# Two-layer hybrid encoder, 1 core: meta queries of mixer D stacked into fewer products, mixer A's sums of squares moved behind the next transpositions, rotation read from SBUF, last columns stored in two pieces

## Chip, cores and metric

The kernel runs on one core of a Trainium2 chip. The metric is the device time of the program in microseconds (us), the median of several executions. TensorE is called PE here, VectorE DVE, ScalarE ACT, GpSimd POOL, SyncE SP.

## What is computed

A trunk of two layers over 272 tokens (16 meta tokens ahead of 256 inputs, whose rows alone are put out) with a width of 1024, all in float32. Cut to what the change touches:

```python
u = rms_norm(h, g_pre)                       # per layer
(a_q, a_k, a_v, b_..., c_..., d_q, d_k, d_v, gate_logits) = split(u @ w_in)
# A: differential attention, 4 heads of 2 x 64, values of 128
#    p = softmax(q k' / 8 + bias), one map per m
#    o = (p[0] - lam * p[1]) @ v ; o = rms_norm(o, subln) * (1 - lam_init)   per head
# B: gated linear attention, in chunks
# C: latent attention, 4 heads of 128 + 64; the 64 are rotated:
#    rope(x) = [x1 * cos - x2 * sin, x1 * sin + x2 * cos]
# D: 8 query heads of 64 on 2 key heads, band of +-128, 16 meta tokens seen by all and seeing all,
#    one sink logit per head
merged = sum_i (branch_i @ w_branch_i) * sigmoid(gate_i)
h = h + rms_norm(merged @ w_out, g_post)
h = h + rms_norm(conv_ffn(rms_norm(h)), g_ffn_post)      # returned: h[:, 16:]
```

## The kernel before, in words

**Products.** Activations lie transposed, 128 features on the partitions and the 272 tokens along the free axis. Every product is made three times on split operands (`mm3`, L305): high times high, high times low, low times high, each part rounded to fp32r. Weights come by DMA on SP's queue as tiles `raw` of 128x1024 (three buffers); ACT rounds each to `wh` and DVE subtracts to get `wl` (both L221), two tiles ahead of their use (five buffers). A projection is a run of 24 matmuls `pj` per 128 output rows, into one of three PSUM banks ("mm").

**Order of work.** Per layer the mixers A, B, C, D follow one another. While one mixer's steps are computed, projections of the next mixer, gates and branch products (`br`) are put between its steps as filling, so many per step by a table. Attention heads are staggered: scores of head h (first half of the queries), transpositions for head h-1, scores of head h (second half), products with the values for head h-1. A Tile scheduler then fixes an order for each engine; each engine works its list in that order, so that a waiting instruction holds all behind it. The other PSUM banks are two for scores ("sc") and three for the rest ("ax": transpositions `tpv`, `tpp`, `tpr`, `tpm`, sums `ps_A`, outputs `poA`). In layer 1 the last layer's unneeded meta rows are left out, so 258 columns instead of 272 stand in many of its instructions.

**Meta queries.** The 16 meta tokens' queries of all heads go through one score tile `scm` (128 rows = heads x 16). For that, `fill_qm` (L584) copies the queries into a zeroed tile, `QM`, high part in `Ah` and low part in `Al` (ACT copy and DVE subtraction, L311 and L312). In D (`comp_d`, L1151) four such blocks are multiplied by `mm3` each: 12 matmuls (L1160 to L1162). The softmaxed rows `pm` are then transposed by `m_transposed` (L645) into `tpm`: three matmuls in float32 against the identity for C and D, where a float32 matmul appears as two records in the trace. All other transpositions (`PE.transpose`, L186) have one record.

**A.** `values(h)` (L947) begins with `head_sums(h-1)`: two matmuls `ps_A` with a matrix of ones that sum the squares of head h-1's outputs, and ACT's copy of them to `aq` (L945). Then come `tpv` (values), `tpp` and `tpr` (maps), ACT's and DVE's splitting of those to `pth`, `ptl`, `ptr`, `vh`, `vl`, `vrA`, and, after filling, the products `poA`. ACT copies `poA` to `av` (L960), squares and rounds it (L520, L521), DVE makes the low part. `scores(h)` (L924) begins with `q_split` of its queries.

**C's rotation.** `rope` (L977) is called for a PSUM bank `qu`: ACT scales the bank to `cq` (L1042), copies four groups of 32 partitions from the bank, swapped and scaled, to `sw` (L983; one buffer), DVE multiplies `sw` by the sines (L984) and `cq` by the cosines (L985), and adds (L986).

**End.** The last down-projection accumulates in four banks `dt`. For the last 128 rows, per half of 512 columns: ACT squares and sums (L1337), DVE multiplies by the gain to `yt` (L1338). Then DVE adds the two sums (L1339), ACT takes Ln and Exp (L1340, L1341, shown as L163), DVE scales and adds the residual per half (L1344), and each half is stored, one from SP's queue, one from ACT's (L1345).

Of the kernel before, what the change touches and what calls it, by code (L numbers as in the profile page):

```python
# [13 lines left out]
F32 = mybir.dt.float32  # L14
F32R = mybir.dt.float32r
AF = mybir.ActivationFunctionType
# [4 lines left out]
P = 128  # L21
# [96 lines left out]
def hybrid_kernel(ctx: ExitStack, tc: tile.TileContext, hT0, w, pc_in, p2_in, cc_in, oh_in, tab_in, gl_in, out):  # L118
# [142 lines left out]
    for nm, wd in (("Ah", 640), ("Al", 640), ("R", P)):  # L261
        QM[nm] = const.tile([P, wd], F32R, name=f"qm{nm}")
        G.memset(QM[nm].bitcast(F32), 0.0)
    keep_warm(N_WARM0)
    PTR = []
    VR = {}
    for i in range(2):
# [205 lines left out]
    for l in range(DEPTH):  # L473
# [9 lines left out]
        with ExitStack() as scope:  # L483
# [161 lines left out]
            def m_transposed(pm, rhs, ncols, name):  # L645
                tm = tmp.tile([P, 3, P], F32, name=name, tag="tm", bufs=1)
                tp = axb("tpm")
                for kc, (k0, n) in enumerate(KC):
                    PE.matmul(tp[:n, kc * ncols:(kc + 1) * ncols], lhsT=pm[:, k0:k0 + n], rhs=rhs, start=True,
                              stop=True)  # L650
                V.tensor_copy(tm[:, 0:2, :ncols], tp[:, :2 * ncols].rearrange("p (a b) -> p a b", a=2))
                V.tensor_copy(tm[:16, 2, :ncols], tp[:16, 2 * ncols:3 * ncols])
                return tm
# [242 lines left out]
            def comp_a(d):  # L896
# [21 lines left out]
                pm, st = softmax_rows(psm, biasMA, -NEG)  # L918
                V.tensor_mul(st[:, 1:2], st[:, 1:2], lamM)
                V.tensor_scalar(pm, pm, st[:, 1:2], None, ALU.mult)  # L920
                yield
                tm, sqs = [], []

                def scores(h, pair):  # L924
                    bias = tmp.tile([P, 2, 400], F32, name="bA", tag="bias")
                    toep(bias, 2 * h, -RMAX, P, 400, [[ROW, 2]])
                    qh, ql = q_split(d["q"][h])
                    for qt in range(2):
                        pp = []
                        for m in range(2):  # L930
                            r = slice(64 * m, 64 * m + 64)
                            qr = slice(128 - 128 * qt, 256 - 128 * qt)
                            ps = scb("sc")
                            mm3(ps[:, :T], qh[r, qr], ql[r, qr], ak[0][h][r, :], ak[1][h][r, :], True, True)
                            off = 128 * (1 - qt)
                            pp.append(softmax_rows(ps, bias[:, m, off:off + T], -NEG))
                        (p0, s0), (p1, s1) = pp
                        V.tensor_mul(s1[:, 1:2], s1[:, 1:2], neglam)
                        V.tensor_scalar(p0, p0, s0[:, 1:2], None, ALU.mult)
                        V.scalar_tensor_tensor(p0, p1, s1[:, 1:2], p0, ALU.mult, ALU.add)  # L940
                        pair.append(p0)
                        yield

                def head_sums(h):
                    S.copy(d["q"][h][:, cs], sum_heads(sqs[h], "A")[:, cs])  # L945

                def values(h, pair):  # L947
                    if h:
                        head_sums(h - 1)
                    else:  # L950
                        tm.append(m_transposed(pm, C("comb"), 64, "tmA"))
                    e = slice(h * P, (h + 1) * P)
                    vh, vl = v_transposed(d["v"][h], VR["A"][:, e])
                    pts = pt_tiles()
                    transpose_p(pts, pair)
                    put_m(pts, tm[0], 16 * h)
                    yield
                    po = axb("poA")
                    pv(po, lambda kc: vh[:, kc, :], lambda kc: vl[:, kc, :], VR["A"][:, e], pts, True, True)
                    S.copy(d["v"][h][:, cs], po[:, cs])  # L960
                    sqs.append(square_hl(d["v"][h]))
# [12 lines left out]
                    yield  # L974


            def rope(dst, src, rows, c0=0, scale=1.0):  # L977

                sw = tmp.tile([P, T], F32, name="sw", tag="sw", bufs=1)
                c = slice(c0, T)  # L980
                for b_ in range(0, rows, 32):
                    o = b_ ^ 32
                    S.activation(sw[b_:b_ + 32, c], src[o:o + 32, c], AF.Copy, scale=scale)  # L983
                V.tensor_mul(sw[:rows, c], sw[:rows, c], C("sin", 0, rows)[:, c])  # L984
                V.tensor_mul(dst[:, c], dst[:, c], C("cos", 0, rows)[:, c])  # L985
                V.tensor_add(dst[:, c], dst[:, c], sw[:rows, c])  # L986

            def proj_c(d, kper):
                lf, sqs = [], []
                for n in (1, 2):  # L990
                    yield from proj_f(n, "cl", lf, None, ct * (n - 1))
                    sqs += [square(f, f"sqc{n}", ct * (n - 1)) for f in lf[n - 1:]]
                rope(kper, kper, 64)
                kp = u("kph", F32R), u("kpl", F32R)
                split(kp[0][0:64, :], kp[1][0:64, :], kper)
                S.copy(kp[0][64:128, :], kper)
                V.tensor_sub(kp[1][64:128, :], kper, kp[0][0:64, :].bitcast(F32))
                d["kp"], d["lat"] = kp, (lf, sqs)
                yield
# [19 lines left out]
            def proj_c_up(d):  # L1019
# [16 lines left out]
                for i in (4, 5, 0, 1, 2, 3):  # L1036
                    ps = mmb("qu")
                    for k in range(2):
                        mm3(ps[:, cs], wq[k][0][:, i * P:(i + 1) * P], wq[k][1][:, i * P:(i + 1) * P], lh[1 + k][:, cs],
                            ll[1 + k][:, cs], k == 0, k == 1)  # L1040
                    qf.append(u(f"cq{i}"))
                    S.activation(qf[-1][:, cs], ps[:, cs], AF.Copy, scale=C_SCALE)  # L1042
                    if i >= 4:
                        rope(qf[-1], ps, P, ct, C_SCALE)
                    if i % 2:
                        yield
                qf[:] = qf[2:] + qf[:2]

            def comp_c(d):
# [43 lines left out]

                def values(h, pair):
                    if not h:
                        tm.append(m_transposed(pm, ident, P, "tmC"))
                    e = slice(h * P, (h + 1) * P)
                    vh, vl = v_transposed(vf[h], VR["A"][:, e])
                    pts = pt_tiles()
# [8 lines left out]
                pairs = [[] for _ in range(4)]  # L1108
                yield from staggered([(scores(h, pairs[h]), values(h, pairs[h])) for h in range(4)])


            def proj_d(d):
                kh, kl = u4("dkh", F32R, 2), u4("dkl", F32R, 2)
# [31 lines left out]
                turn()  # L1145
                d["k"], d["v"], d["q"] = (kh, kl), vp, [u("dq0")]
                evac(dq0, d["q"][0], RS, 0.125, ct)
                yield
                yield from proj_f(3, "dq", d["q"], 0.125, ct)

            def comp_d(d):  # L1151
                dq, (kh, kl), vp = d["q"], d["k"], d["v"]
                clear_qm(0)
                fill_qm("A", dq, 160, 2)
                d["br"] = br = branch_tiles("brD")
                vr = VR["D"].rearrange("p (a b) -> p a b", a=2)
                nsink = sm.tile([P, 9], F32, name="nsink", tag="nsink", bufs=1)
                V.tensor_scalar(nsink, PCc("sink", 0, 9), -1.0, None, ALU.mult)
                psm = scb("scm")
                for j in range(4):  # L1160
                    mm3(psm[:, :T], QM["Ah"][:, j * P:(j + 1) * P], QM["Al"][:, j * P:(j + 1) * P], kh[j // 2],
                        kl[j // 2], j == 0, j == 3)  # L1162
                pm, st = softmax_rows(psm, biasMD, nsink[:, 8:9], sink=PCc("sinkM"))
                V.tensor_scalar(pm, pm, st[:, 1:2], None, ALU.mult)
                yield
                tm, qs, pos = [], [], []

                def scores(hd, pair):
                    j, par = divmod(hd, 2)
                    if not par:  # L1170
                        qs[:] = q_stack(dq[j])
                    kv = hd // 4
                    bias = tmp.tile([P, 2, 400], F32, name="bD", tag="bias")
                    toep(bias[:, :, 0:16], 16 + hd, -271, P, 16, [[128, 2]])
# [1 line left out]
                    for qt in range(2):  # L1176
                        qr = slice(128 - 128 * qt, 256 - 128 * qt)
                        ps = scb("sc")
                        stacked(ps[:, :T], qs[par][:, qr], kh[kv], kl[kv], True, True)
                        p, st = softmax_rows(ps, bias[:, 1 - qt, :T], nsink[:, hd:hd + 1], sink=PCc("sink", hd))  # L1180
                        V.tensor_scalar(p, p, st[:, 1:2], None, ALU.mult)
                        pair.append(p)
                        yield

                def values(hd, pair):
                    j, par = divmod(hd, 2)
                    kv = hd // 4
                    if not hd:
                        tm.append(m_transposed(pm, ident, P, "tmD"))
                    pts = pt_tiles()  # L1190
                    transpose_p(pts, pair)
                    put_m(pts, tm[0], 16 * hd)
# [79 lines left out]
        with tc.tile_pool(name=f"ffn{l}", bufs=1, reuse_waits="tile") as ffn:  # L1272
# [34 lines left out]
            def down_rows():  # L1307
# [17 lines left out]
                for t in range(2):  # L1325
# [3 lines left out]
                    for n in range(2):  # L1329
# [5 lines left out]
                            PE.matmul(ps, lhsT=ah[:, kk, c], rhs=ws[1][:, e], start=False, stop=kk == NF - 1)  # L1335
                        sq = ffn.tile([P, 512], F32, name="sqt", tag="sqt", bufs=2)
                        S.activation(sq, ps, AF.Square, accum_out=st[:, n:n + 1])  # L1337
                        V.tensor_mul(y[:, e], ps, gl[:, e])  # L1338
                    V.tensor_add(st[:, 2:3], st[:, 0:1], st[:, 1:2])  # L1339
                    act(LN_EXP_SET, st[:, 3:4], st[:, 2:3], AF.Ln, scale=1.0 / DM, bias=epst)  # L1340
                    act(LN_EXP_SET, st[:, 3:4], st[:, 3:4], AF.Exp, scale=-0.5)  # L1341
                    for n in range(2):
                        e = slice(512 * n, 512 * n + 512)
                        V.scalar_tensor_tensor(y[:, e], y[:, e], st[:, 3:4], ht[:, t, e], ALU.mult, ALU.add)  # L1344
                        (nc.sync, S)[n].dma_start(out[P * t:P * t + P, e], y[:, e])  # L1345

            ah = ffn.tile([P, NF, T], F32R, name="ah")
            al = ffn.tile([P, NF, T], F32R, name="al")
# [209 lines left out]
```

## Time and profile before

| what | value |
| --- | --- |
| times of three runs | 1138.22, 1136.12, 1136.78 us; median 1136.78 |
| the profiled execution | 1137.86 us, of which the span from first to last instruction is 1136.1 |
| granted clock of TensorE, mean | 0.999 |
| busy in the span | PE 98%, DVE 81%, ACT 67%, POOL 1% |
| weights and other data moved | 183.73 MB, mean 162 GB/s |

The profiled execution took 1.8 us more than its span, and 1.1 us more than the median of the three runs. "Busy" of PE counts overlapping matmuls: while PE runs without a gap, a matmul of 272 columns has a duration of 0.29 us in the trace, but the next one starts 0.125 us later. So the worth of a matmul is read from starts, not from durations.

### The profile page before, as it was taken

The numbers are of one execution on the slowest core, as the hardware profiler recorded it, in microseconds if no ns is written. First come the engines' busy times: TensorE is split into PE (matmuls) and PEld (weight loads), VectorE is DVE, ScalarE is ACT, GpSimd is POOL, SyncE is SP. The second block draws the span as 40 slices with busy tenths as digits, with TensorE's granted clock in tenths as the row PEclk, the third lists the DMA queues.
The fourth block names the chain that finished last, engine by engine and source line by source line (L and its number), as shares of the span: only waits on it lengthen the run. The fifth ranks groups of instructions, "written<-read, shape, count | busy, mean of one in ns | idle before, by whom it ended". The sixth has DMA issues, their size and how long they took to land.

```text
span 1136.1 us, 22808 instructions
## 1 busy us (share of the span) xinstructions
PE 1113.3 (98%) x8678; PEld 1077.5 (95%) x8678; DVE 918.8 (81%) x2001; ACT 760.9 (67%) x1623; POOL 12.8 (1%) x57
## 2 busy tenths in 40 slices
PE   9999999999999999999999999999999999999997
PEld 8999899999999999999999998999999999999986
DVE  6977986898976899995479868868989759999843
ACT  7756787777755767664457557867777657766632
POOL 1000000000000000000000000000000000000000
PEclk9999999999999999999999999999999999999999
DMA  7643444445656356655546434644466472655551
GB/s 266 217 149 117 132 149 149 131 130 135 168 149 214 105 173 202 183 165 175 181 143 214 149 114 126 159 154 136 139 146 173 150 244 93 208 201 186 186 188 71
DMA packets 60914, 183.73 MB, mean 162 GB/s; under 512 B 10443, under 2 KB 17739, under 8 KB 60420
## 3 DMA queue, kind: packets, MB, share of 16 engines
q1 hardware_dynamic: 60148, 181.36, 51.8%
q8 instruction: 68, 1.11, 0.4%
q10 hardware_dynamic: 656, 0.91, 0.2%
q14 instruction: 42, 0.34, 0.1%
HBM read 180.03 MB, written 2.21 MB: 160 GB/s over the span
## 4 chain that ended last, share of the span: by engine, by line
PE 77%; DVE 9%; ACT 8%; DMA 3%; issue 2%; DVEq 0%; SPq 0%; ACTq 0%
PE pj L183 49%; PE br L183 7%; PE dn L183 6%; PE dt L183 5%; DMA raw<-wst 3%; DVE wl L221 2%; ACT wh L221 2%; PE poD L183 1%; PE sc L183 1%; PE poB L183 1%; PE at L183 1%; PE tpp L186 1%; ACT p L607 1%; ACT sw L983 1%; PE kvu L183 1%
## 5 line engine op out<-in xcount | busy, mean ns | idle before, releaser
L183 PE MATMUL pj<-xh,wh 128*128 128x272 f32 (+1 forms) x1888 | 547.2, 292 | 6.4 <-ACT xh L350 3.1
L183 PE MATMUL pj<-xl,wh 128*128 128x272 f32 (+1 forms) x1888 | 540.6, 287 | 0.0
L183 PE MATMUL pj<-xh,wl 128*128 128x272 f32 (+1 forms) x1888 | 540.3, 287 | 0.0
L221 DVE TENSOR_TENSOR wl<-raw,wh 128x1024 fp32r<-128x1024 f32 (+2 forms) x322 | 387.1, 1205 | 111.4 <-ACT wh L221 108.5
L221 ACT CAST wh<-raw 128x1024 fp32r<-128x1024 f32 (+2 forms) x322 | 332.7, 1035 | 198.5 <-PE pj L183 90.8
L183 PEld LDWEIGHTS pj<-xh,wh 128*128 128x128 f32 x1888 | 354.7, 189 | 12.1 <-ACT xh L350 3.7
L183 PEld LDWEIGHTS pj<-xl,wh 128*128 128x128 f32 x1888 | 356.6, 189 | 1.8 <-issue 0.4
L183 PEld LDWEIGHTS pj<-xh,wl 128*128 128x128 f32 x1888 | 355.9, 189 | 0.2
L1365 ACT ACTIVATE cv<-u,pc 128x272 f32<-128x272 f32 (+1 forms) x88 | 52.9, 606 | 15.2 <-DVE u L1363 15.0
L183 PE MATMUL dn<-ah,wh 128*128 128x272 f32 x176 | 51.0, 290 | 0.0
L183 PE MATMUL dn<-al,wh 128*128 128x272 f32 x176 | 50.7, 288 | 0.0
L183 PE MATMUL dn<-ah,wl 128*128 128x272 f32 x176 | 50.5, 287 | 0.0
L607 ACT ACTIVATE p<-p,st 128x272 f32<-128x272 f32 x68 | 35.1, 516 | 14.6 <-DVE st L605 14.5
L1369 DVE SCALAR_TENSOR_TENSOR cv<-u,pc,cv 128x271 f32<-128x271 f32 (+1 forms) x88 | 43.0, 490 | 1.8
L1367 DVE SCALAR_TENSOR_TENSOR cv<-u,pc,cv 128x271 f32<-128x271 f32 (+1 forms) x88 | 42.9, 488 | 1.0 <-ACT cv L1365 0.6
L1210 DVE TENSOR_TENSOR gt<-pj,rs_x 128x272 f32<-128x272 f32 (+1 forms) x64 | 27.6, 431 | 15.2 <-PE pj L183 14.3
L1363 DVE TENSOR_TENSOR u<-pj,rs_x 128x272 f32<-128x272 f32 (+1 forms) x88 | 36.9, 426 | 0.0
L183 PE MATMUL dt<-wh,al 128*128 128x512 f32 x88 | 34.8, 395 | 0.0
L183 PE MATMUL dt<-wh,ah 128*128 128x512 f32 x88 | 34.7, 395 | 0.0
L183 PE MATMUL dt<-wl,ah 128*128 128x512 f32 x88 | 34.5, 392 | 0.0
L183 PEld LDWEIGHTS dn<-ah,wh 128*128 128x128 f32 x176 | 33.1, 188 | 0.0
L183 PEld LDWEIGHTS dn<-al,wh 128*128 128x128 f32 x176 | 33.1, 188 | 0.0
(390 smaller groups left out, 1894.1 us busy)
## 6 DMA issues: line engine op xcount, KB each, us to landing
raw<-wst SPq DMA_DIRECT2D x306, 512.0 KB, 3.7
raw<-wst SPq DMA_DIRECT2D x12, 384.0 KB, 3.2
bD<-bvec SPq DMA_DIRECT2D x16, 256.0 KB, 5.1
bA<-bvec SPq DMA_DIRECT2D x8, 400.0 KB, 5.7
hT<-hT SPq DMA_DIRECT2D x1, 1088.0 KB, 6.3
h_dram<-hT SPq DMA_DIRECT2D x1, 1088.0 KB
hT<-h_dram SPq DMA_DIRECT2D x1, 1088.0 KB, 6.1
raw<-wst SPq DMA_DIRECT2D x4, 256.0 KB, 4.6
```

The source lines that it names most:

```text
L183: self.note(nc.tensor.matmul(*args, **kw))
L186: self.note(nc.tensor.transpose(*args, **kw))
L221: pair = S.copy(wh[:, c], raw[:, c]), V.tensor_sub(wl[:, c], raw[:, c], wh[:, c].bitcast(F32))
L607: S.activation(p, p, AF.Exp, scale=-1.0, bias=st[:, 0:1], accum_out=st[:, 1:2])
L983: S.activation(sw[b_:b_ + 32, c], src[o:o + 32, c], AF.Copy, scale=scale)
L1210: V.tensor_mul(f[:, ct:T], (yield from pj(ct))[:, ct:T], RS[:, ct:T])
L1363: V.tensor_mul(u_[:, ct:T], ps[:, ct:T], RS[:, ct:T])
L1365: S.activation(t[:, cd:T], u_[:, cd:T], AF.Identity, scale=PCc("cw1", c), bias=PCc("cb", c))
L1367: V.scalar_tensor_tensor(t[:, lo:T], u_[:, lo - 1:T - 1], PCc("cw0", c), t[:, lo:T], ALU.mult, ALU.add)
L1369: V.scalar_tensor_tensor(t[:, cd:T - 1], u_[:, cd + 1:T], PCc("cw2", c), t[:, cd:T - 1], ALU.mult, ALU.add)
```

## The change

It has five parts.

1. D's meta queries are stacked: the high and the low part of a query lie above each other in one 128-row block (`QS`, 128 columns of the tile `QM` that were not used), one block for each key head. `meta_q` fills it after each of the four query projections, in place of `fill_qm` at the start of `comp_d`; `stacked` multiplies a block with the high and with the low keys: 4 matmuls instead of 12 per layer.
2. `m_transposed` uses `PE.transpose` for C and D.
3. A's `head_sums(h-1)` goes from the start of `values(h)` to just ahead of `poA`; `q_split` in A and `q_stack` in D are issued a step earlier.
4. `rope` reads `cq`, which lies in SBUF, instead of the PSUM bank.
5. In the end part, the sums are added ahead of the second multiplication by the gain, which is issued after Ln and Exp; the last 512 columns of the last rows are stored as two pieces of 256.

```diff
+    QS = [QM[nm][:, 512:640] for nm in ("Ah", "Al")]
...
                 for kc, (k0, n) in enumerate(KC):
-                    PE.matmul(tp[:n, kc * ncols:(kc + 1) * ncols], lhsT=pm[:, k0:k0 + n], rhs=rhs, start=True,
-                              stop=True)
+                    o = tp[:n, kc * ncols:(kc + 1) * ncols]
+                    if rhs is None:
+                        PE.transpose(o, pm[:, k0:k0 + n], ident)
+                    else:
+                        PE.matmul(o, lhsT=pm[:, k0:k0 + n], rhs=rhs, start=True, stop=True)
...
+                qs = [q_split(d["q"][0])]
                 yield
...
-                    qh, ql = q_split(d["q"][h])
+                    qh, ql = qs.pop()
...
                         pair.append(p0)
+                        if qt and h < 3:
+                            qs.append(q_split(d["q"][h + 1]))
                         yield
...
                 def values(h, pair):
-                    if h:
-                        head_sums(h - 1)
-                    else:
+                    if not h:
                         tm.append(m_transposed(pm, C("comb"), 64, "tmA"))
...
                     put_m(pts, tm[0], 16 * h)
                     yield
+                    if h:
+                        head_sums(h - 1)
                     po = axb("poA")
...
-                    S.activation(sw[b_:b_ + 32, c], src[o:o + 32, c], AF.Copy, scale=scale)
+                    S.copy(sw[b_:b_ + 32, c], dst[o:o + 32, c])
...
+            def meta_q(dq, j):
+
+                for m in range(2):
+                    o = 16 * (2 * (j % 2) + m) + 64 * (j // 2)
+                    oc, t = slice(o, o + 16 - ct), QS[j // 2]
+                    r, r2 = slice(64 * m, 64 * m + 64), slice(64 - 64 * m, 128 - 64 * m)
+                    src = dq[j][r, 15:ct - 1 if ct else None:-1]
+                    S.copy(t[r, oc], src)
+                    V.tensor_sub(t[r2, oc], src, t[r, oc].bitcast(F32))
...
-                yield from proj_f(3, "dq", d["q"], 0.125, ct)
+                for j in range(1, 4):
+                    yield from proj_f(1, f"dq{j}_", d["q"], 0.125, ct)
+                    meta_q(d["q"], j)
...
-                for j in range(4):
-                    mm3(psm[:, :T], QM["Ah"][:, j * P:(j + 1) * P], QM["Al"][:, j * P:(j + 1) * P], kh[j // 2],
-                        kl[j // 2], j == 0, j == 3)
+                for kv in range(2):
+                    stacked(psm[:, :T], QS[kv], kh[kv], kl[kv], kv == 0, kv == 1)
...
-                        V.tensor_mul(y[:, e], ps, gl[:, e])
-                    V.tensor_add(st[:, 2:3], st[:, 0:1], st[:, 1:2])
-                    act(LN_EXP_SET, st[:, 3:4], st[:, 2:3], AF.Ln, scale=1.0 / DM, bias=epst)
+                        if n:
+                            V.tensor_add(st[:, n:n + 1], st[:, n:n + 1], st[:, n - 1:n])
+                        if not n:
+                            V.tensor_mul(y[:, e], ps, gl[:, e])
+                    act(LN_EXP_SET, st[:, 3:4], st[:, n:n + 1], AF.Ln, scale=1.0 / DM, bias=epst)
                     act(LN_EXP_SET, st[:, 3:4], st[:, 3:4], AF.Exp, scale=-0.5)
-                    for n in range(2):
-                        e = slice(512 * n, 512 * n + 512)
+                    V.tensor_mul(y[:, e], ps, gl[:, e])
+                    for n, (c0, c1) in enumerate(((0, 512), (512, 768), (768, DM)) if t else ((0, 512), (512, DM))):
+                        e = slice(c0, c1)
                         V.scalar_tensor_tensor(y[:, e], y[:, e], st[:, 3:4], ht[:, t, e], ALU.mult, ALU.add)
-                        (nc.sync, S)[n].dma_start(out[P * t:P * t + P, e], y[:, e])
+                        (nc.sync, S, nc.sync)[n].dma_start(out[P * t:P * t + P, e], y[:, e])
```

Where the instructions go, in three places.

PE's list before, around the meta scores of D in layer 0 (`dkh_3235` and `dkl_3237` are the high and low keys of the first key head, `qmAh` and `qmAl` the parts of the queries, `pj` a projection that fills):

```order
L183 MATMUL scm<-dkh_3235,qmAl 128x272
L183 MATMUL scm<-dkh_3236,qmAh 128x272
L183 MATMUL scm<-dkl_3238,qmAh 128x272
L183 MATMUL scm<-dkh_3236,qmAl 128x272
L183 MATMUL scm<-dkh_3236,qmAh 128x272
L183 MATMUL scm<-dkl_3238,qmAh 128x272
L183 MATMUL scm<-dkh_3236,qmAl 128x272
L183 MATMUL pj<-xh,wh 128x272
```

The same place after the change, in full:

```order
L183 MATMUL pj<-xh,wl 128x272
L183 MATMUL scm<-dkh_3235,qmAh 128x272
L183 MATMUL scm<-dkl_3237,qmAh 128x272
L183 MATMUL pj<-xh,wh 128x272
L183 MATMUL pj<-xl,wh 128x272
L183 MATMUL scm<-dkh_3236,qmAl 128x272
L183 MATMUL scm<-dkl_3238,qmAl 128x272
L183 MATMUL pj<-xh,wl 128x272
```

Of 12 matmuls in one block 4 are left, in two pairs with two filling matmuls between them.

PE's list before, at the last head of A in layer 1 (`br` is a branch product that fills):

```order
L183 MATMUL br<-brBh_9034,wh 128x258
L183 MATMUL ps_A<-sq,ones_r 128x258
L186 MATMUL tpv<-cc,av_9091 128x128 x2
L186 MATMUL tpv<-cc,av_9091 16x128
L183 MATMUL ps_A<-sq,ones_r 128x258
L186 MATMUL tpp<-cc,p 128x128 x4
L183 MATMUL br<-brBl_9035,wh 128x258
L183 MATMUL br<-brBh_9034,wl 128x258
L186 MATMUL tpr<-cc,p 16x128 x2
```

The same place after the change, from the end of the third head's `poA` on: 12 filling matmuls (the last two are shown), then the transpositions.

```order
L183 MATMUL br<-brBl_9027,wh 128x258
L183 MATMUL br<-brBh_9026,wl 128x258
L186 MATMUL tpv<-cc,av_9083 128x128 x2
L186 MATMUL tpv<-cc,av_9083 16x128
L186 MATMUL tpp<-cc,p 128x128 x4
L186 MATMUL tpr<-cc,p 16x128 x2
L183 MATMUL br<-brBh_9020,wh 128x258
```

The `ps_A` pair has left this place (it now stands directly ahead of the next `poA`), the transpositions follow one another, and before them stand 12 filling matmuls instead of 22.

ACT's list before, around C's rotation in layer 0 (`cq_2759` and `cq_2776` are the two rotated query tiles, `gt` a gate):

```order
L163 ACTIVATE gt_2694<-gt_2694 128x272
L1042 ACTIVATE cq_2759<-qu 128x272
L983 ACTIVATE sw<-qu 32x272 x4
L1042 ACTIVATE cq_2776<-qu 128x272
L983 ACTIVATE sw<-qu 32x272 x4
L163 ACTIVATE gt_2786<-gt_2786 128x272
L1042 ACTIVATE cq_2827<-qu 128x272
L221 CAST wh<-raw 128x1024
L1042 ACTIVATE cq_2836<-qu 128x272
```

After the change:

```order
L163 ACTIVATE gt_2694<-gt_2694 128x272
L1049 ACTIVATE cq_2759<-qu 128x272
L1049 ACTIVATE cq_2776<-qu 128x272
L990 COPY sw<-cq_2759 32x272 x4
L221 CAST wh<-raw 128x1024
L990 COPY sw<-cq_2776 32x272 x4
L163 ACTIVATE gt_2786<-gt_2786 128x272
L1049 ACTIVATE cq_2827<-qu 128x272
L1049 ACTIVATE cq_2836<-qu 128x272
```

Both copies out of PSUM now come first, and a weight cast stands between the two groups of four.

More of the change, by code (lines that the diff above doesn't have):

```diff
@@ L974, in comp_a, with rope @@
                     yield
-            def rope(dst, src, rows, c0=0, scale=1.0):
+            def rope(dst, rows, c0=0):
                 sw = tmp.tile([P, T], F32, name="sw", tag="sw", bufs=1)
@@ L992, in proj_c @@
                     sqs += [square(f, f"sqc{n}", ct * (n - 1)) for f in lf[n - 1:]]
-                rope(kper, kper, 64)
+                rope(kper, 64)
                 kp = u("kph", F32R), u("kpl", F32R)
@@ L1043, in proj_c_up @@
                     if i >= 4:
-                        rope(qf[-1], ps, P, ct, C_SCALE)
+                        rope(qf[-1], P, ct)
                     if i % 2:
@@ L1095, in values @@
                     if not h:
-                        tm.append(m_transposed(pm, ident, P, "tmC"))
+                        tm.append(m_transposed(pm, None, P, "tmC"))
                     e = slice(h * P, (h + 1) * P)
@@ L1147, in proj_d @@
                 evac(dq0, d["q"][0], RS, 0.125, ct)
+                meta_q(d["q"], 0)
                 yield
-                yield from proj_f(3, "dq", d["q"], 0.125, ct)
+                for j in range(1, 4):
+                    yield from proj_f(1, f"dq{j}_", d["q"], 0.125, ct)
+                    meta_q(d["q"], j)
             def comp_d(d):
@@ L1153, in comp_d @@
                 clear_qm(0)
-                fill_qm("A", dq, 160, 2)
                 d["br"] = br = branch_tiles("brD")
@@ L1159, in comp_d @@
                 psm = scb("scm")
-                for j in range(4):
-                    mm3(psm[:, :T], QM["Ah"][:, j * P:(j + 1) * P], QM["Al"][:, j * P:(j + 1) * P], kh[j // 2],
-                        kl[j // 2], j == 0, j == 3)
+                for kv in range(2):
+                    stacked(psm[:, :T], QS[kv], kh[kv], kl[kv], kv == 0, kv == 1)
                 pm, st = softmax_rows(psm, biasMD, nsink[:, 8:9], sink=PCc("sinkM"))
                 V.tensor_scalar(pm, pm, st[:, 1:2], None, ALU.mult)
+                tm, qs, pos = [], q_stack(dq[0]), []
                 yield
-                tm, qs, pos = [], [], []
                 def scores(hd, pair):
                     j, par = divmod(hd, 2)
-                    if not par:
-                        qs[:] = q_stack(dq[j])
                     kv = hd // 4
@@ L1182, in scores @@
                         pair.append(p)
+                        if par and qt and j < 3:
+                            qs[:] = q_stack(dq[j + 1])
                         yield
@@ L1188, in values @@
                     if not hd:
-                        tm.append(m_transposed(pm, ident, P, "tmD"))
+                        tm.append(m_transposed(pm, None, P, "tmD"))
                     pts = pt_tiles()
```

## The prediction, made before the changed kernel ran

> **What bounds the kernel now.** I read the page first: the busy times and the chain that ended last.
>
> ```profile
> PE 1113.3 (98%) x8678; PEld 1077.5 (95%) x8678; DVE 918.8 (81%) x2001; ACT 760.9 (67%) x1623; POOL 12.8 (1%) x57
> ...
> PE 77%; DVE 9%; ACT 8%; DMA 3%; issue 2%; DVEq 0%; SPq 0%; ACTq 0%
> ```
>
> PE is busy for 1113.3 of 1136.1 us, and the chain runs through PE for 77%. There are two ways to gain: take matmuls away where PE runs without a gap, or close one of the gaps, which are 1136.1 - 1113.3 = 22.8 us in all. So next I read what PE waited for, and there the rows at instructions that the change touches (total us, times, longest):
>
> ```profile
> PE tpr L186 <- ACT aq L945: 1.4, 3, 0.8
> PE pj L183 <- DVE gt L1210: 1.3, 2, 0.7
> ...
> PE ps_A L183 <- ACT sq L521: 0.6, 2, 0.4
> PE poC L183 <- DVE ptl L312: 0.6, 2, 0.3
> ...
> PE pj L183 <- ACT sw L983: 0.3, 1, 0.3
> ```
>
> The change addresses 1.4 + 0.6 us in A (the sums of squares) and 1.3 + 0.3 us around C's rotation; no more than these 3.6 us, plus the refilling of PE after each, can come from closed gaps. Whether a removed matmul counts depends on the stage. The windows are C's and D's attention in layer 0, then both in layer 1 (length; busy of PE, PEld, DVE, ACT, POOL; granted clock; DMA share; GB/s):
>
> ```profile
> 209.00:256.00 47.00, 45.70 (x359) 43.97 (x358) 42.77 (x110) 34.38 (x93) 0.27 (x2) 1.00 0.45 134
> 256.00:326.00 70.00, 70.00 (x562) 69.19 (x561) 61.75 (x177) 50.85 (x138) 0.00 (x0) 1.00 0.59 152
> 777.00:825.00 48.00, 46.80 (x379) 45.18 (x378) 44.90 (x113) 34.53 (x94) 0.28 (x2) 1.00 0.44 141
> 825.00:890.00 65.00, 65.00 (x543) 64.20 (x542) 58.92 (x173) 49.77 (x134) 0.00 (x0) 1.00 0.60 157
> ```
>
> D is purely PE: 70.00 of 70 and 65.00 of 65 us. In C, PE has gaps and DVE is at 42.77/47 = 91% and 44.90/48 = 94%: there DVE sets part of the pace, and time taken off PE may only lengthen PE's waits.
>
> **1. D's meta scores.** The block of 12 in layer 0 and the filling matmul behind it, and the last DVE write of D's meta queries:
>
> ```profile
> 256.88 0.29 PE L183 MATMUL scm<-dkh,qmAh 128*128 128x272 f32 x1
> ...
> 258.38 0.29 PE L183 MATMUL pj<-xh,wh 128*128 128x272 f32 x1
> ```
> ```profile
> 257.24 0.36 DVE L312 TENSOR_TENSOR qmAl<-dq,qmAh 64x16 fp32r<-64x16 f32 x2
> ```
>
> (258.38 - 256.88)/12 = 0.125 us per matmul; eight fewer are 1.0 us per layer, 2.0 in both, all on the path since PE has no gap in D. Against it: the last block is complete at 257.24 + 0.36 = 257.60. Before, the tenth matmul was the first to need the last projection's queries; now the second pair needs them as PE's fifth instruction from the block's start, at 256.88 + 4 x 0.125 = 257.38. That is a wait of 0.22 us per layer, with everything on PE behind it. 2 x (1.0 - 0.22) = 1.56; I take **1.5**. Bounds: 2.0 without the wait, 0.5 if the pair waits about half a microsecond longer in each layer. The numbers of ACT's and DVE's small copies stay (8 and 8 per layer); they move ahead, into the projections, where the DVE of C is nearly full, which I count in part 3's caution for C.
>
> **2. Transposed meta rows.** In D of layer 0:
>
> ```profile
> 265.18 0.93 PE L183 MATMUL tpm<-cc,p 128*128 128x128 f32 x6
> 266.04 0.66 PE L186 MATMUL tpp<-cc,p 128*128 128x128 f32 x4
> 266.54 0.38 PE L186 MATMUL tpr<-cc,p 128*16 128x128 f32 x2
> ```
>
> Three float32 products (six records) take 266.04 - 265.18 = 0.86 us. Four transpositions of the same 128 columns take 266.54 - 266.04 = 0.50, or 0.125 each, so three are 0.375 and the gain is 0.485 per place. In D it is kept, since the maps that follow are not waited for: 2 x 0.485, **1.0** (0.5 to 1.0). In C it is worth that only where DVE's backlog leaves it, and the row of `poC` waiting for `ptl` (0.6) says that it mostly doesn't: **0.2** (0 to 1.0).
>
> The Trainium skill, in "TensorE: Matmul & The Clock Gate", section Terms, gives the transpose mode as four times as fast for float32. By it the 0.86 would fall to 0.215, and the sum below would be 0.3 us larger in D; the row of `tpp` speaks for 0.375.
>
> **3. Sums of squares behind the transpositions.** Before, the `ps_A` pair stands ahead of `tpv`, waits for ACT's squares, and holds a bank until ACT has copied it to `aq`; `tpr` gets that bank. The longest case, in layer 1:
>
> ```profile
> 703.90 0.28 PE L183 MATMUL pj<-xh,wh 128*128 128x258 f32 x1
> 704.94 0.39 PE L186 MATMUL tpr<-cc,p 128*16 128x128 f32 x2 [0.76 <-ACT aq L945]
> ```
>
> From start to start it is 1.04; less one matmul of 0.12 the hole is 0.92 us, 0.16 more than the 0.76 shown as idle, which is the refilling of PE. The five waits are 1.4 + 0.6 + 5 x 0.16 = 2.8 us. Moved to just before `poA`, the pair comes a whole step later: the squares and the copy are then done. What is late next? At the last head the transpositions now follow the third `poA` after 12 filling matmuls instead of 22. In layer 1, that `poA`'s last matmul, ACT, and DVE's last step of the map to be transposed are:
>
> ```profile
> 720.20 0.28 PE L183 MATMUL poA<-ptr,vrA 128*128 128x258 f32 x1
> ```
> ```profile
> 719.26 1.28 ACT L154 ACT_TABLE_LOAD   x1
> 720.56 0.52 ACT L607 ACTIVATE p<-p,st 128x272 f32<-128x272 f32 x1
> ```
> ```profile
> 722.10 0.50 DVE L940 SCALAR_TENSOR_TENSOR p<-p,st 128x272 f32<-128x272 f32 x1
> ```
>
> The map is finished at 722.60, behind a table load of 1.28 us on ACT. PE, earlier by 1.0 or so for the closed gaps, passes 13 matmuls at 0.12 and three transpositions at 0.125 after 719.2, and reaches `tpp` at about 721.1. If ACT and DVE stay where they are, that is a new wait of 1.5 us. Sum 2.8 - 1.5 = **1.3**. Bounds: 2.8 if the map comes earlier with the scores, 0 if the new wait, with one like it in layer 0, eats all. `q_split` and `q_stack` a step ahead: nothing, as no row has PE waiting for them.
>
> **4. Rotation from SBUF.** ACT's second group of four copies in layer 0, DVE's multiplication, the weight split after it, the gate that PE waits for, and the copies by their source:
>
> ```profile
> 196.95 1.59 ACT L983 ACTIVATE sw<-qu 32x272 f32<-32x272 f32 x4 [0.92 <-DVE cq L986]
> ```
> ```profile
> 198.57 0.44 DVE L984 TENSOR_TENSOR sw<-sw,cc 128x272 f32<-128x272 f32 x1 [1.20 <-ACT sw L983]
> ```
> ```profile
> 200.39 1.23 DVE L221 TENSOR_TENSOR wl<-raw,wh 128x1024 fp32r<-128x1024 f32 x1 [0.89 <-ACT wh L221]
> ```
> ```profile
> 203.52 0.44 DVE L1210 TENSOR_TENSOR gt<-pj,rs_x 128x272 f32<-128x272 f32 x1
> ```
> ```profile
> L983 ACT ACTIVATE sw<-qu x16: 375/384/392, 194.0 to 767.8; 32x272 f32<-32x272 f32 x8, 32x258 f32<-32x258 f32 x8
> ...
> L983 ACT ACTIVATE sw<-t x4: 429/430/430, 29.9 to 602.9; 32x272 f32<-32x272 f32 x4
> ```
>
> ACT stood 0.92 us before the second group (one `sw` buffer), DVE 1.20 and then 0.89 us: the `wh` cast came behind both groups. Now the bank is free after one copy, so the 0.3 us of `pj` behind `sw` goes, and the cast fills ACT's gap between the groups; DVE's `wl` goes into the 1.20 us. The gate comes earlier by the 0.89 that `wl` waited, less the price of the copies. From SBUF (`t`) they take 430 ns, from PSUM (`qu`) 384: 4 x 0.046 = 0.2 us for the second group. About 0.7 earlier, which is the longest wait for `gt`. With the refilling the three waits are 1.3 + 0.3 + 3 x 0.16 = 2.1 us; I take **1.5** (0.3 to 2.1).
>
> The Trainium skill speaks against this part: "Advanced Engine Details and Errata", The Read-Write Bubble, has ScalarE closer to PSUM and VectorE closer to SBUF. The rows of 384 and 430 ns agree in sign; that price is in the sum.
>
> **5. The end.**
>
> ```profile
> 1129.85 0.69 DVE L1338 TENSOR_TENSOR yt<-dt,gl 128x512 f32<-128x512 f32 x1 [2.07 <-ACT sqt L1337]
> 1130.46 0.15 DVE L1339 TENSOR_TENSOR st<-st 128x1 f32<-128x1 f32 x1
> 1131.20 1.41 DVE L1344 SCALAR_TENSOR_TENSOR yt<-yt,st,ht 128x512 f32<-128x512 f32 x2 [0.60 <-ACT st L163]
> ```
> ```profile
> 1130.64 0.29 ACT L163 ACTIVATE st<-st,epst 128x1 f32<-128x1 f32 x1 [0.83 <-DVE st L1339]
> 1130.97 0.20 ACT L163 ACTIVATE st<-st 128x1 f32<-128x1 f32 x1
> ```
> ```profile
> out<-yt ACTq DMA_DIRECT2D x1, 256.0 KB, 2.1
> ```
>
> The addition moves from 1130.46 to 1129.85, and Ln and Exp with it. The multiplication (0.69) then runs beside them, 1130.00 to 1130.69, and the scaling starts there instead of at 1131.20: 0.5 earlier. It costs 0.70 for the first half, and the 272-column step above (0.50) bounds each quarter: done at 1132.4 or a little before, against 1132.61, so 0.2 to 0.5 is kept. The last store is half as large: between nothing and 1.0 of its 2.1 us; I take 0.2, since a fixed share can't be told apart here. Together **0.6** (0.2 to 1.5).
>
> **Sum.** 1.5 + 1.0 + 0.2 + 1.3 + 1.5 + 0.6 = 6.1 us. The profiled execution took 1137.86 (span 1136.1 and 1.8 around it): 1131.8 after. The runs' median is 1136.78, so the forecast is 1136.78 - 6.1 = 1130.7.
>
> **The rivals.**
>
> *Everything lands:* no new wait in A, none in C, none at the stacked pair. 2.0 + 1.0 + 1.0 + 2.8 + 2.1 + 1.5 = 10.4, so 1126.4. For it: every gap is in the waits. Against it: DVE at 91 to 94% in C, and the map at 722.60.
>
> *DVE sets the pace:* PE arrives earlier and waits longer, so that A, C and the rotation give nothing. Left are 1.5 + 1.0 + 0.6 = 3.1, so 1133.7. For it: DVE's 44.90 of 48; against it, PE has no gap in D, where a lead could be kept.
>
> *The stacked pair waits for a whole weight split:* if DVE takes another `wl` (1.23) ahead of the last block, part 1 gives 2 x (1.0 - 0.22 - 1.23), about -0.9 instead of 1.5, and the time is 1133.1.
>
> *Slower:* the `ps_A` pair and `poA` behind it now both need banks that DVE empties (`ptl`, `vrA`), at three heads in each layer, six places. A late DVE there holds PE's whole list, filling included. About 30 filling matmuls, 3.6 us, lie between. The forecast falls to no gain at 6.1/6 = 1.0 us of wait per place, and to 1139.9 at 1.5 us. DVE would have to be two splits of 1.23 late each time; no such wait (`poA` for `ptl`) is among the rows now.
>
> **How the numbers follow.** Forecast 0.50 (1128.5 to 1132.5 by itself), everything lands 0.12, DVE's pace 0.27, pair waits 0.07, slower 0.04. A measurement can tell about 0.2% from no change, 2.3 us: 1134.5 and 1139.1 are the borders. Of DVE's pace a fifth to a quarter lies above 1134.5, and most of the slower case's paths end near no change or beyond: faster 0.88, same 0.09, slower 0.03. The range, 1126.4 to 1134.6, leaves out half of the first rival, a fifth of the second and the last, some 0.15.
>
> **What would show it.** Right: four `scm` in D, 0.5 us of PE's time plus a wait under 0.3; `tpm` to `tpp` in 0.4; no row of `tpr` behind `aq`; a wait of `tpp` for `p` of about 1.5 at the end of A in layer 1; no row of `pj` behind `sw` and less behind `gt`; D's windows still full. Wrong: `poA` or `ps_A` waiting for `ptl` or `vrA` by over 1 us, or new rows of `tpv` and `poC` in C as large as the gains.

## The result and the profile after

The changed kernel takes 1131.51 us (median of 5 runs, 1130.35 to 1132.06) against 1136.78 before (5 runs, 1136.12 to 1138.22): 5.3 us less, a ratio of 0.9947 with a 95% interval of 0.9936 to 0.9958. The forecast was 1130.7. The profiled execution took 1131.75 us, its span was 1130.0.

First the page of the changed kernel, busy times and the chain:

```profile
PE 1107.8 (98%) x8650; PEld 1073.8 (95%) x8650; DVE 919.3 (81%) x2002; ACT 760.3 (67%) x1623; POOL 12.8 (1%) x57
...
PE 85%; DVE 7%; ACT 5%; DMA 2%; issue 1%; SPq 0%; DVEq 0%; ACTq 0%
```

PE's busy time fell by 5.5 us, and its gaps (span less busy) from 22.8 to 22.2 only. So nearly all of the gain looks like work taken away, though the change also aimed at gaps. PE's waits show why:

```profile
PE tpv L186 <- DVE vpl L313: 1.9, 4, 0.9
...
PE poC L183 <- DVE ptl L313: 0.9, 2, 0.7
PE tpp L186 <- ACT aq L952: 0.9, 1, 0.9
PE pj L183 <- DVE gt L1228: 0.6, 2, 0.4
PE ps_A L183 <- ACT sq L522: 0.6, 2, 0.4
...
PE scm L183 <- DVE qmAl L1127: 0.4, 2, 0.2
...
PE tpp L186 <- DVE p L945: 0.2, 1, 0.2
```

`tpr` behind `aq` (1.4) and `pj` behind `sw` (0.3) are gone, `pj` behind `gt` fell from 1.3 to 0.6. New are `tpp` behind `aq` (0.9) and behind `p` (0.2) and `scm` behind `qmAl` (0.4); `ps_A` behind `sq` stands at 0.6 as before, at other places, and `tpv` and `poC` in C wait for DVE by 0.7 more.

Since whole times scatter by more than most terms of the sum, I cut each trace at PE's first instruction of each kind and compared the stages (us; in the column of the changed kernel the difference to before):

| stage, from first instruction to first instruction | before | changed |
| --- | --- | --- |
| start to A's `scm`, layer 0 | 106.78 | 105.60 (-1.17) |
| A: `scm` to C's `kvu`, layer 0 / 1 | 72.97 / 71.90 | 72.83 (-0.14) / 71.90 (0.00) |
| rotation: `kvu` to C's `scm` | 28.91 / 28.00 | 28.11 (-0.80) / 26.96 (-1.03) |
| C: `scm` to D's `scm` | 48.23 / 46.78 | 47.74 (-0.49) / 47.12 (+0.34) |
| D: `scm` to `ps_post` | 113.92 / 109.13 | 112.83 (-1.09) / 108.01 (-1.13) |
| rest of layer 0 and B of layer 1 | 307.19 | 307.51 (+0.32) |
| rest of layer 1 to PE's last matmul | 194.89 | 194.91 (+0.02) |
| PE's last matmul to the end | 7.37 | 6.44 (-0.93) |

`kvu` is C's up-projection, `ps_post` the sum of squares behind the mixers. A gained nothing, and the largest single difference lies at the start, where PE, ACT and DVE work the same lists before and after; only two ACT copies there (`sw<-t`, of C's key rotation) have another opcode.

### The profile page after: what moved, and what is told of

The parts are those of the page before. It is cut to its first block, busy times and chain, and to the rows that moved or that the text cites. A ratio compares the mean times of both kernels' runs of the same rounds, so it can differ in the third digit from the quotient of the medians.

```text
span 1130.0 us, 22748 instructions
## 1 busy us (share of the span) xinstructions
PE 1107.8 (98%) x8650; PEld 1073.8 (95%) x8650; DVE 919.3 (81%) x2002; ACT 760.3 (67%) x1623; POOL 12.8 (1%) x57
## 4 chain that ended last, share of the span: by engine, by line
PE 85%; DVE 7%; ACT 5%; DMA 2%; issue 1%; SPq 0%; DVEq 0%; ACTq 0%
PE pj L183 56%; PE br L183 6%; PE dn L183 6%; PE dt L183 5%; DVE wl L221 2%; PE sc L183 2%; ACT wh L221 1%; PE poD L183 1%; DMA raw<-wst 1%; PE poB L183 1%; PE at L183 1%; PE tpp L186 1%; PE kvu L183 1%; DMA p<-p 1%; PE d L183 0%
```

## The experiments

The theory after this look: the matmuls taken from D count, less the wait at the second stacked pair; the rotation counts in full; A's part only moved its waits to two places where the filling runs out; the start is scatter. The rivals are in the expectations.

**e1. The kernel before, once more** (no edit).

> The kernel before, unchanged, profiled once more. Question: is the 1.17 us that the changed kernel gained ahead of mixer A's meta scores in layer 0 (105.60 against 106.78 us), where the change touches nothing on PE, an effect of the change or a scatter of the first weight loads? Theory (scatter): the start of those scores falls anywhere between 105.4 and 106.9 us here, and the later stages keep their lengths within 0.15 us (72.97 for A, 28.91 for the rotation stage, 48.23 for C, 113.92 for D of layer 0). Rival (the change does it, by the other instruction for the copies of the first rotation): it stays at 106.8 within 0.2.

Measured: 1137.91 us; start 107.00; A 72.32 and 71.98; rotation 28.91 and 27.96; C 48.31 and 47.17; D 113.92 and 109.16; end 7.35. The rotation, D and the end repeat within 0.05. A of layer 0 (0.65 less than in the first profile) and C of layer 1 (0.39 more) do not, against the 0.15 of the theory: there a single difference of some tenths means nothing. The start fits the rival (106.8 within 0.2) and lies just above the theory's span; e4, e8 and e9 below say more.

**e2 and e3. A's part undone in the changed kernel, and alone in the kernel before.** The edit, undone and made:

```diff
 def values(h, pair):
-    if h:
-        head_sums(h - 1)
-    else:
+    if not h:
         tm.append(m_transposed(pm, C("comb"), 64, "tmA"))
...
     yield
+    if h:
+        head_sums(h - 1)
     po = axb("poA")
```

with `q_split` a step ahead as in the change.

> The changed kernel with A's part undone (sums of squares ahead of the transpositions again, queries split in their own step). Theory (the A part only moved its waits: to the transposition of the last head in layer 1 and to the last sums in layer 0): A's stages return to about 73.0 and 71.9 us, so 0.1 and 0.0 longer, and the time is that of the changed kernel within 0.3 us, 1131.5. Rival (the forecast: A's part is worth 1.3): A's two stages are longer by 1.3 together, time 1132.8.

> The kernel before with A's part alone. Theory (the waits moved within A): the stages of A are 72.8 and 71.9 us, as in the changed kernel, everything behind as before; time 1136.6. Rival (A's part gains 1.3 by itself and the other parts take it away): 72.3 and 71.3, time 1135.5.

Measured: undone 1131.97 us (4 runs, 1130.56 to 1132.69), A's stages 72.33 and 71.71. Alone 1136.85 (10 runs) against 1137.05, ratio 1.000 (0.999 to 1.0009), stages 72.12 and 71.90. The time of e3 fits the theory, and its interval leaves out the rival (1135.5, a ratio of 0.9986). The time of e2 lies 0.5 from the theory and 0.8 from the rival and decides little, but A's stages did not grow by 1.3. Layer 0's 72.12 in e3 would fit the rival, but the kernel before itself had 72.32 in e1, so one stage decides nothing. Over five profiles with the part as in the change (after, e3, e6, e7, e8) the stages average 72.32 and 71.89, over five without it (before, e1, e2, e4, e9) 72.46 and 71.79: no gain that can be told.

**e4. Rotation alone in the kernel before.**

```diff
-    S.activation(sw[b_:b_ + 32, c], src[o:o + 32, c], AF.Copy, scale=scale)
+    S.copy(sw[b_:b_ + 32, c], dst[o:o + 32, c])
```

> The kernel before with the rotation from SBUF alone. Theory: the stage from C's up-projection to its meta scores shortens by 0.8 in layer 0 (28.91) and 1.0 in layer 1 (28.00), as in the changed kernel, since no other part touches it; nothing else moves; time 1135.0. Rival (part of it is due to A's work being done earlier): half of that, 1135.9.

Measured: 1135.23 us (10 runs) against 1137.05, ratio 0.9987 (0.9977 to 0.9996); the stage is 28.12 and 26.96, shorter by 0.79 and 1.04, to 0.02 what the whole change gives. The theory held. The start is 107.34, with the same two `sw<-t` copies as in the changed kernel: the rival of e1 is out.

**e5, e10, e11, e12. More filling in A.** A step more ahead of the last head's transpositions and one more ahead of the last sums; then each alone (`N_A` is (25, 30)); then both with A's part undone.

```diff
-N_A = (24, 30)
+N_A = (26, 30)
...
+        for _ in range(late):        # late=1 for A
+            yield
         next(before)
...
     yield from staggered(...)
     yield
+    yield
     head_sums(3)
```

> The changed kernel with two more steps in A's order, one ahead of the last head's transpositions and one ahead of the last sums of squares, so that more filling stands before both (the same filling, spread over 26 steps instead of 24). Theory (the A part's gain was given back at these two places, where the filling ran out): the waits there, 0.29 and 0.93 us in layer 0 and 1.46 and 0.58 in layer 1, mostly go; A's stages are 0.9 and 1.5 us shorter than in the changed kernel (72.83 and 71.90), time 1129.2. Rival (ACT and DVE set A's pace, whatever the order): the waits come back at other heads and the stages stay within 0.4 us, time 1131.3.

> The changed kernel with one more step in A, ahead of the last head's transpositions alone. Theory (in layer 1 the wait stands there, 1.46 us; in layer 0 mostly at the last sums): A's stage is 0.5 to 0.8 shorter in layer 1 (71.89), 0 to 0.3 in layer 0 (71.95 to 72.83), time 1130.5. Rival (the last sums are the place, which come from the same late ACT): no change, 1131.5.

> The changed kernel with one more step in A, ahead of the last sums of squares alone. Theory: the waits of 0.93 us (layer 0) and 0.58 (layer 1) there go; A's stages 0.2 to 0.9 and 0.2 to 0.4 shorter, time 1130.7. Rival: they only move behind it, to the queries' projections of C; no change, 1131.5.

> Both additional steps, with A's part of the change undone. Question: is the gain with the two steps (1129.23 against 1131.51) one of the steps alone? Theory (A's part frees the bank early, the steps give the cover that it lacked; both are needed): half of the gain at most, A's stages 72.0 and 71.6, time 1130.6. Rival (the steps alone): 71.8 and 71.2 as with A's part, time 1129.3.

| kernel | time (runs) | A, layer 0 / 1 |
| --- | --- | --- |
| changed | 1131.51 (1130.35 to 1132.06) | 71.95 to 72.83 / 71.90 |
| A's part undone (e2) | 1131.97 (1130.56 to 1132.69) | 72.33 / 71.71 |
| both steps | 1129.23 (1128.56 to 1129.47) | 71.79 / 71.22 |
| last head only | 1133.39 (1132.85 to 1134.11) | 73.63 / 72.32 |
| last sums only | 1132.02 (1131.49 to 1132.90) | 73.40 / 71.44 |
| both steps, A's part undone | 1131.16 (1130.60 to 1132.94) | 71.88 / 72.10 |

Both steps gave the time of the theory, and a version that beats both kernels: its four runs all lie below the five of the changed kernel. The ratio to before is 0.9929 (0.9912 to 0.9945), an interval that still touches the changed kernel's. The time agreed partly by luck, since A's stage of layer 1 gave 0.7 of the 1.5 expected. But the steps singly went against my expectation: with the last head's alone the time rose by 1.9 us. In its profile A's stages are 1.3 and 0.4 longer than the averages of e3, and the end is 0.6 longer (see e8). Its PE timeline at the last head, in layer 0 and in layer 1:

```profile
154.25 0.28 PE L183 MATMUL br<-brBh,wh 128*128 128x272 f32 x1
155.70 0.52 PE L183 MATMUL ps_A<-sq,ones_r 128*128 128x272 f32 x2 [1.16 <-DVE ptl L313]
```
```profile
721.97 0.28 PE L183 MATMUL br<-brBh,wh 128*128 128x258 f32 x1
723.64 0.50 PE L183 MATMUL ps_A<-sq,ones_r 128*128 128x258 f32 x2 [1.39 <-DVE ptl L313]
```

The waits at the transpositions are gone, but filling put ahead of them is missing behind them: the `ps_A` pair comes up for the bank that DVE has not emptied yet, and waits 1.16 and 1.39 us. That is the mechanism of the forecast's slower rival, at two of its six places. With the last sums alone the same row has 1.1 us in layer 0, and in layer 1 `tpp` still waits 0.6 for the map; that kernel's time can't be told from the changed one's. Only with both steps (spread over 26) does the filling fit in both halves; then one such wait of 0.8 is left. With A's part undone the same steps leave layer 1 at 72.10: the part is worth some 0.9 us there, but only under more cover. Read as a square, the table says the same: without the part and the steps 1131.97, with the part alone 1131.51, with the steps alone 1131.16, and only with both 1129.23. The time with the steps alone is nearer its theory (1130.6) than its rival (1129.3). Of the 2.3 us between the changed kernel and the one with both steps, A's stages show 0.5 and 0.7 (against the averages 72.32 and 71.89). Another 0.5 lies in the rest of layer 1 (194.40) and isn't due to the steps: e6, which has none of them, has it too (194.44), and e12, which has both, doesn't (195.03). The remainder is start and scatter.

**e6. D's scores a step later.**

```diff
+                yield
                 psm = scb("scm")
...
-N_D = (35, 36)
+N_D = (36, 36)
```

> The changed kernel with one more step ahead of D's stacked meta scores, so that 12 filling matmuls come first (36 steps of filling instead of 35). Theory (the second stacked pair waits for DVE's last low part of the meta queries, 0.40 and 0.35 us from start to start): both waits vanish, D's stages are 0.3 to 0.4 us shorter each (112.83 and 108.01), time 1130.8. Rival (the wait only moves, to the transpositions of the meta rows, which now follow the scores sooner): no change within 0.1 in either stage, 1131.5.

Measured: 1133.00 us (5 runs, 1132.80 to 1134.51), 1.5 slower than the changed kernel. C's and D's stages must be taken together here, since the mark itself moved: 160.98 against 160.57, and 156.49 against 155.13. The row of `scm` behind `qmAl` is gone, and this one came:

```profile
PE poD L183 <- DVE ptl L313: 1.0, 2, 0.6
```

So the rival was nearer, but even it was too kind: what was won at the pair (0.40 and 0.35) was lost more than once over. In layer 0 the new wait (0.41 of the 1.0, plus refilling) and one of 0.12 at a `tpp` behind it cover most of the loss; in layer 1 (0.58 and 0.11) they cover only part, and where the rest goes stays open.

**e7. C's meta rows by matmul again.**

```diff
-    tm.append(m_transposed(pm, None, P, "tmC"))
+    tm.append(m_transposed(pm, ident, P, "tmC"))
```

> The changed kernel with C's meta rows transposed by matmuls again, as before. Theory (DVE sets C's pace, so that the 0.5 us taken from PE are kept in layer 0 only): C's stage is 0.4 to 0.6 longer in layer 0 (47.74) and within 0.2 in layer 1 (47.12). Rival (the transpositions count in full): 0.5 longer in both. Second question, the start: the meta scores of A in layer 0 began at 105.6 in two runs with the other parts of the change and at 106.8 to 107.5 in four without them; if that is scatter, this run and its neighbours fall outside 105.6 as well.

Measured: 1131.42 us (one run). C's stage is 48.56 in layer 0 (47.64 to 47.77 in seven profiles with the transpositions) and 47.06 in layer 1 (47.08 to 47.21). So the 0.5 taken from PE are worth 0.85 in layer 0 and nothing that can be told in layer 1. PE's rows show why. In layer 0 the version with matmuls has a wait that the changed kernel hasn't (e7):

```profile
234.43 0.36 PE L183 MATMUL poC<-pth,vh 128*128 128x272 f32 x1 [0.31 <-DVE ptl L313]
```

In layer 1 the lead of 0.5 us is kept up to one transposition and lost there, since DVE isn't ready earlier. First the changed kernel, then e7:

```profile
805.94 0.33 PE L186 MATMUL tpv<-cc,pf 128*128 128x128 f32 x1 [0.89 <-DVE vpl L313]
```
```profile
805.61 0.33 PE L186 MATMUL tpv<-cc,pf 128*128 128x128 f32 x1 [0.27 <-DVE vpl L313]
```

So there one of the forecast's signs of being wrong did show: a wait of `tpv` in C as large as the gain.

**e8. The last store in halves again.**

```diff
-for n, (c0, c1) in enumerate(((0, 512), (512, 768), (768, DM)) if t else ((0, 512), (512, DM))):
+for n, (c0, c1) in enumerate(((0, 512), (512, DM))):
```

> The changed kernel with the last 512 columns stored in one piece again, the earlier addition and the later multiplication kept. Between PE's last matmul and the end there were 7.37 us before and 6.44 after. Theory (the earlier addition gives 0.5, the two pieces the rest): 6.85. Rival A (the pieces bring nothing, a store has a fixed price): 6.45. Rival B (the pieces bring most): 7.2.

Measured: 1131.82 us (one run); the end takes 6.75 (nearest to the theory), of which 3.70 pass until the last store is issued and 3.05 behind that. Before it was 4.30 and 3.07: the earlier addition gives 0.60. In the changed kernel, with pieces, it is 3.80 and 2.64: 0.1 later, and 0.4 shorter behind. That 0.4 is not steady: in e10 and e11 the end took 7.01, with the same rows up to the issue. The last stores of the changed kernel, and then of e10 (the last figure is the time from issue to landing):

```profile
out<-yt ACTq DMA_DIRECT2D x1, 128.0 KB, 2.0
out<-yt SPq DMA_DIRECT2D x1, 128.0 KB, 2.0
```
```profile
out<-yt ACTq DMA_DIRECT2D x1, 128.0 KB, 2.6
out<-yt SPq DMA_DIRECT2D x1, 128.0 KB, 2.6
```

This run also bears on the start: 106.80, with nearly the whole change in it.

**e9. Stacked scores alone in the kernel before** (`QS`, `meta_q` and `stacked` as in the change, nothing else).

> The kernel before with D's stacked meta scores alone. Theory (eight matmuls less, 1.0 us, minus the wait for the last low part, 0.40 from start to start less its cover): D's stages are 0.6 us shorter each (113.92 and 109.13), nothing else moves but the chance of the start, time 1135.8. Rival (the small copies moved into C's projections cost DVE as much there): C's stages 0.3 to 0.5 longer, time 1136.7.

Measured: 1136.01 us (10 runs) against 1136.94, ratio 0.9995 (0.9986 to 1.0005): the time alone can't tell it from nothing. D's stages are 113.43 and 108.54, shorter by 0.49 and 0.59; C's 48.39 and 47.11 are those of e1 within 0.1. In layer 0 the rival is out, as five kernels with C's meta rows by matmul as before lie at 48.23 to 48.42; in layer 1 they scatter from 46.78 to 47.57, too much to tell. And the start, with all other parts out, is 105.88: it scatters with and without the change. But of nine profiles with most of the change seven lay at 105.4 to 106.1, and of five without it four lay above 106.7, so that a part of the 1.17 us could be an effect; what would cause it stays open.

## Why the prediction was right, and where it was not

The total came out within 0.8 us and by the forecast's main case. A's term was wrong, and C's, which gave more than forecast, made up for half of it, which is luck.

**1. D's meta scores: 1.5 forecast, 1.1 measured** (e9). PE's timeline there, changed kernel, layer 0:

```profile
254.28 0.29 PE L183 MATMUL scm<-dkh,qmAh 128*128 128x272 f32 x1
254.40 0.29 PE L183 MATMUL scm<-dkl,qmAh 128*128 128x272 f32 x1
254.53 0.29 PE L183 MATMUL pj<-xh,wh 128*128 128x272 f32 x1
254.65 0.28 PE L183 MATMUL pj<-xl,wh 128*128 128x272 f32 x1
255.18 0.40 PE L183 MATMUL scm<-dkh,qmAl 128*128 128x272 f32 x1 [0.24 <-DVE qmAl L1127]
255.41 0.29 PE L183 MATMUL scm<-dkl,qmAl 128*128 128x272 f32 x1
255.54 0.29 PE L183 MATMUL pj<-xh,wl 128*128 128x272 f32 x1
```

The wait was found where it was put, and its idle time is 0.24 (0.22 forecast). From start to start it costs 255.18 - 254.65 - 0.125 = 0.40, and the next matmul comes 0.10 late as well. The failing step is the 0.22 itself: I counted PE's refilling of 0.16 in parts 3 and 4 and left it out here. The rival, a whole `wl` ahead of the last block, did not happen.

**2. Transposed meta rows: 1.2 forecast, 2.0 measured.** The same place as before:

```profile
262.09 0.49 PE L186 MATMUL tpm<-cc,p 128*128 128x128 f32 x3
262.42 0.60 PE L186 MATMUL tpp<-cc,p 128*128 128x128 f32 x4
262.86 0.38 PE L186 MATMUL tpr<-cc,p 128*16 128x128 f32 x2
```

0.33 us for three, instead of 0.86: 0.53 gained (0.485 forecast), and D's stages less the stacked scores leave 1.09 - 0.49 = 0.60 and 1.13 - 0.59 = 0.54. The forecast's 0.125 for each is an average with a slower first one (0.16, then 0.11 each). The factor is 0.86/0.33 = 2.6. By the factor of four in the Trainium skill ("TensorE: Matmul & The Clock Gate", Terms) the estimate would have been 0.215 us, and this trace does not bear it out. C, taken as 0.2, gave 0.85 in layer 0 and 0 in layer 1 (e7): the share left by DVE's backlog was mis-sized.

**3. A: 1.3 forecast, nothing measured.** The forecast's new wait at the last head of layer 1 is there, changed kernel, first PE, then ACT and DVE:

```profile
717.06 0.49 PE L186 MATMUL tpv<-cc,av 128*128 128x128 f32 x3
718.45 0.44 PE L186 MATMUL tpp<-cc,p 128*128 128x128 f32 x2 [0.89 <-ACT aq L952]
719.12 0.44 PE L186 MATMUL tpp<-cc,p 128*128 128x128 f32 x2 [0.24 <-DVE p L945]
```
```profile
715.72 1.28 ACT L154 ACT_TABLE_LOAD   x1
717.02 0.52 ACT L608 ACTIVATE p<-p,st 128x272 f32<-128x272 f32 x1
717.45 0.19 ACT L608 ACTIVATION_READ_ACCUMULATOR p<-p,st 128x1 f32 x1
717.54 0.51 ACT L608 ACTIVATE p<-p,st 128x272 f32<-128x272 f32 x1
717.95 0.19 ACT L608 ACTIVATION_READ_ACCUMULATOR p<-p,st 128x1 f32 x1
718.04 0.35 ACT L952 COPY aq<-ps_A 128x258 f32<-128x258 f32 x1
```
```profile
718.57 0.50 DVE L945 SCALAR_TENSOR_TENSOR p<-p,st 128x272 f32<-128x272 f32 x1
```

Its size is 1.06 + 0.40 = 1.46 us with refilling (1.5 forecast), in two pieces. The piece that ends last waits for the map, finished at 719.07 behind the table load, as forecast. The piece before it waits for ACT's copy of the sums, behind the same table load and the exponentials, so that "the squares and the copy are then done" wasn't true at this head; but by these rows the map alone would have held PE until the same 719.1. What failed is the rest of the term: I put the last sums at nothing, and they are the second place. Those of layer 0, again PE and then ACT:

```profile
157.31 0.28 PE L183 MATMUL br<-brBh,wl 128*128 128x272 f32 x1
158.01 0.87 PE L183 MATMUL ps_A<-sq,ones_r 128*128 128x272 f32 x2 [0.42 <-ACT sq L522]
```
```profile
154.03 2.00 ACT L221 CAST wh<-raw 128x1024 fp32r<-128x1024 f32 x2
155.93 0.38 ACT L952 COPY aq<-ps_A 128x272 f32<-128x272 f32 x1
156.20 0.39 ACT L967 COPY av<-poA 128x272 f32<-128x272 f32 x1
```

PE reached the last `poA` at 153.53 instead of 155.58, 0.9 us earlier if the 1.17 of the start is taken off. Then two weight casts (2.00 us) stood on ACT ahead of the copy of `poA`, the squares came late, and PE lost 0.58 + 0.35 at the sums. In layer 1 the same place costs 0.38, and the last head of layer 0 costs 0.29. The new waits are thus 1.46 + 0.93 + 0.38 + 0.29 = 3.1 us, where the forecast had 1.5; they take back all of the 2.8 that were closed. A lead on PE is kept only if what releases it next moves too; e5 shows that it is kept when filling covers both places.

**4. Rotation: 1.5 forecast, 1.8 measured** (0.79 + 1.04, e4). ACT's list in the changed kernel, and then PE's remaining wait:

```profile
192.27 0.77 ACT L1049 ACTIVATE cq<-qu 128x272 f32<-128x272 f32 x2
193.07 1.70 ACT L990 COPY sw<-cq 32x272 f32<-32x272 f32 x4
195.48 1.05 ACT L221 CAST wh<-raw 128x1024 fp32r<-128x1024 f32 x1 [0.71 <-PE pj L183]
196.56 1.71 ACT L990 COPY sw<-cq 32x272 f32<-32x272 f32 x4
```
```profile
201.91 0.39 PE L183 MATMUL pj<-xh,wh 128*128 128x272 f32 x1 [0.27 <-DVE gt L1228]
```

The cast stands between the groups as forecast, and the gate's wait fell from 0.61 to 0.27 in layer 0 and from 0.71 to 0.37 in layer 1. The price of the copies was over-sized: a copy of `cq` takes 412 ns against 384 from PSUM, 28 more and not 46. That isn't the source alone, since the copy is another instruction now (COPY in place of ACTIVATE): for `sw<-t`, which read SBUF before and after, it brought 430 down to 418. At equal width and instruction (272 columns, ACTIVATE) the source made 430 against 389. The rule of the Trainium skill ("Advanced Engine Details and Errata", The Read-Write Bubble) holds in sign, and did not decide.

**5. The end: 0.6 forecast, 0.93 measured** in most runs, 0.36 in two. The early addition gave 0.60 where I kept 0.2 to 0.5; the pieces gave 0.3 or lost 0.3 by the landing of their stores.

The terms measured are 1.1 + 2.0 + 0 + 1.8 + 0.9 = 5.8 us, against 6.1 forecast and 5.3 between the medians; the half microsecond is within what the start scatters. One sum of the forecast is off without consequence: the slower rival's six places at 1.5 us give 1130.7 + 9.0 = 1139.7, not 1139.9.

## What to carry to other kernels

Price a moved instruction at each place that it is moved to, and look where the filling ends: work taken off a stalled engine comes back as a wait at the next place with too little cover, here the last head and the last sums. Filling is a budget, and the steps have to be given out again when an order changes: one step more made the kernel slower at one place and no faster at the other, and only both together made it faster than the kernels before and after. Add the refilling of PE to each new wait, also to the short ones. And where terms are tenths of a microsecond, compare stages of traces: the stacked scores alone were invisible in 10 runs' times and plain in two stages.

## What was not expected of the hardware

The start varies: the first matmul of A's meta scores came at 105.4 to 107.5 us over fourteen profiles of kernels whose lists are alike up to there, and at 105.4 to 106.8 over the nine with most of the change. The end varies too, 128 KB stores landing 2.0 us after their issue in the changed kernel and 2.6 us in e10, with the same rows ahead. A float32 transposition takes PE 0.11 us against 0.29 for the float32 matmul with the identity.
